# Where the Fourier branch's output weights are prepared: beside the last gates through DRAM, or at the start of attention

## The chip, the cores and the metric

The kernel runs on one core of a Trainium2 chip. The metric is the device time of one execution in microseconds. A core has TensorE (PE, matmuls), VectorE (DVE), ScalarE (ACT), GpSimd (POOL) and SyncE (SP, which here only issues transfers). Each engine works through its own list of instructions in order and waits for others on semaphores; 16 DMA engines move data between DRAM and the on-chip memory.

## The reference

One layer of a backbone block on 2048 latent tokens (a grid of 32 by 64) of 1024 channels, with 256 context tokens, in float32. Cut to what matters here:

```
fx, qx, kx, vx = split_projection(hx @ w_in)        # 4 groups of 128 channels; 8 heads of 64
y_four = fft2(fx over tokens and a group's channels, norm="ortho").real
y_attn = neighbourhood_attention(qx, kx, vx, kc, vc, rpb)   # 8 x 16 window, and all 256 context keys
g_f, g_a = split(sigmoid(hx @ w_branch_gate))
merged = g_f * (y_four @ w_fourier_out) + g_a * (y_attn @ w_attn_out)
x = x + g1 * (merged @ w_out)
x = x + g2 * (relu(hx2 @ w_mlp1) ** 2 @ w_mlp2)
```

Of the real part of a two-dimensional transform only half has to be computed: the value at (token, channel) is tied to that at the mirrored place. The kernel therefore needs w_fourier_out in two combinations, the sum and the difference of its rows with its mirrored rows. Each is split into a rounded part and the rest (H and L), so that three fast matmuls give the accuracy of a slow one.

## The kernel before

**Stages.** By the trace: the input projections, with queries, keys, values and gates (to 838 us), the Fourier transform along channels and tokens (838 to 890), attention (890 to 1214) with the Fourier branch's output product beside it, the attention branch's output product and w_out (to 1482), and the MLP (1482 to 2659).

**The gates.** `run_pair(n)` runs the projections of a pair of column blocks; the last pairs are gates. `unit_T` makes eight accumulations in PSUM (`ps_g`); ScalarE applies the sigmoid (`ot_g`, line 516, two buffers, tag "ot") and SyncE stores each result to DRAM (`gT`, line 517). Between the matmuls `turn` advances a generator, `fourier_prep`, by some steps: `pace[0]` says how many, 3 for the last pair (line 768). The generator's last part squares and sums weights (`wn`, line 883), then calls `fold(1)`.

**The Fourier stage.** `channel_dft` multiplies the channels by a folded matrix (`pc`, line 939) and splits the result (`gH`, `gL`); ScalarE's copies `gH` stand behind the last `ot_g` in its list. Matrices of the sequence transform and its input `X` are loaded by SyncE (line 814).

**Attention.** 128 blocks of 128 queries: four head pairs (hp), four row blocks (rb), four column blocks (cb), two heads (h2). Names such as `sc1_2` give the row and column block, with the head in front in the code. A block is: scores on TensorE (`sc`, lines 1303 and 1306), bias and minimum on VectorE (`s`, line 1312), the exponential on ScalarE (1316), transposes on TensorE (`tp`, 1325), two roundings (`pH` on ScalarE, 1328, `pL` on VectorE, 1333) and the product with the values (`pv`, 1339). `issue_after` fixes the order on TensorE, VectorE and ScalarE as the code is written.

**The filler.** After each block from the third on, a generator `beside_attention` is advanced one step, and a second step after every fourth block from block 16 on. It runs `merge_fourier`, then `load_wa`, and, from a fixed block on, `attn_out(0)`. `merge_fourier` first prepares the weights (`load_w`, `ws`, and the splits, lines 1183 to 1215), splits the transform's results (`ya`, `yb`), does a matmul with a single output row (`pr`), turns the row into a column (`puc`), and then does 32 accumulations of six or seven matmuls (`pmf`, line 1263), a step for every two matmuls; the results go to DRAM as `mF`, stored by GpSimd. `load_wa` loads w_attn_out in four pieces (`wao`, tag "wst" with two buffers); GpSimd scales each and splits it into `wa` (lines 1393 to 1395). `attn_out(0)` multiplies the first 256 tokens (`pua`).

**SyncE's queue.** Every load of attention goes through `fetch`, which chains it behind the one before, so that the order is that of the code:

```
    def fetch(dst, src):
        with tc.issue_after(in_order[0].ins):
            in_order[0] = sp.dma_start(dst, src)
```

`prefetch(n)` asks for the queries (`Q`, `Ql`), keys (`k`), values (`vt`) and bias tables (`bt`, issued by GpSimd, line 1091) some blocks ahead. A load that waits for its buffer holds all that stand behind it.

Of the kernel before, what the change touches and what calls it, by code (L numbers as in the profile page):

```python
# [8 lines left out]
F32 = mybir.dt.float32  # L9
# [54 lines left out]
def dit_block(ctx: ExitStack, tc: tile.TileContext, a, out, taps=None, upto=9):  # L64
# [46 lines left out]
    y64 = scratch("y64", [4, 1024])  # L111

    wfr = scratch("wfr", [4, 63, D])
    mF = scratch("mF", [8, 128, S])
    yA = scratch("yA", [4, 128, S])
    x1d = scratch("x1d", [S, D])
# [648 lines left out]
        return r  # L765

    def run_pair(n):
        pace[0] = 3 if n == len(seq) - 1 else (0, 3, 2)[min(n, 2)]
        wu, new = pair(n), [load_pair_unit(n + 1, u) for u in range(2)] if n + 1 < len(seq) else []
        js = [0, 1, "c", 2, 3] if n else [1, 2, 3]  # L770
        for j in js:
            tk = S if j == "c" else j * 512
            parts = []
            for u, (kind, _, _, i) in enumerate(seq[n]):
                if j == "c" and kind not in "kv":
                    continue
                nm = f"{kind}{i}{j}"
                if kind == "f":
                    parts.append(unit_T(wu[u], hx[j], fT, 2 * i, tk, AF.Copy, nm))
                elif kind == "g":  # L780
                    parts.append(unit_T(wu[u], hx[j], gT, 2 * i, tk, AF.Sigmoid, nm))
                elif kind in "qk":
                    parts.append(unit_qk(wu[u], hx[j], kind, 2 * i, tk, None if j == "c" else 4 * j, nm))
                else:
                    parts.append(unit_v(wu[u], hx[j], i, tk // 128, nm))
            mixed = seq[n][0][0] in "qk"
            for u, part in enumerate(parts):
                if mixed:

                    for i, _ in enumerate(part):  # L790
                        if i % 2 and len(parts) > 1:
                            next(parts[1], None)
                else:
                    for _ in part:
                        turn(0)
                if n == 0 and u == 0 and j < 3:
                    if j == 1:
                        hx[0] = first_tokens()
                    xh = [load_x(x2, ((j + 1) * 4 + i) * 128, f"{j + 1}{i}", None, i >= 2, i >= 2) for i in range(4)]
                    hx[j + 1] = build(hx_room(f"hx{j + 1}"), xh, AB, f"{j + 1}")  # L800

            for _ in range((0, 1, 2)[j] if n == 0 and j in (1, 2) else j in (0, 1, 2)):
                for o in new:
                    next(o, None)
# [61 lines left out]
    def fourier_prep():  # L866
        fold(0)
        yield
        for i in range(4):
            tH, tL = (fb.tile([128, 4, 512], F32R, tag=f"t{o}{i}", name=f"t{o}{i}") for o in "HL")  # L870
            tabs.append((tH, tL))

            tw = pa.tile([128, 4, 512], F32, tag="wst", name=f"tw{i}", bufs=2)
            sp.dma_start(tw, a["seq"][i].rearrange("(j p) m -> p j m", p=128))
            for j in range(4):
                split_on((pool, dve)[j % 2], tH[:, j], tL[:, j], tw[:, j])
                yield
            for j in (2 * i, 2 * i + 1):
                w, k = ((a["w_attn_out"][0], j), (a["w_out"][0], j - 2), (a["w_fourier_out"][0], j - 6))[(j >= 2) + (j >= 6)]
                tn = pa.tile([128, 2, D], F32, tag="wst", name=f"wn{j}", bufs=2)  # L880
                sp.dma_start(tn, w[k * 256:(k + 1) * 256, :].rearrange("(k p) n -> p k n", p=128))
                tn = tn.rearrange("p k n -> p (k n)")
                act.activation(tn, tn, AF.Square, accum_out=wn[:, j:j + 1])
                yield
        fold(1)

    for n in range(len(seq)):
        if n == 1:
# [279 lines left out]
    def merge_fourier():  # L1168
# [11 lines left out]
        ws = [pairs("wp"), pairs("wd")]  # L1180
        ys = [pairs("ya"), pairs("yb")]

        def load_w(p, fetch):
            w, wm, t = (stage(f"w{o}{p}") for o in "fms")
            for h in range(2):
                o, r0 = 64 * h, (2 * p + h) * 128
                fetch(w[o:o + 64], wf[r0:r0 + 64, :])
                pool.memset(wm[o:o + 1], 0.0)
                fetch(wm[o + 1:o + 64], wfr[2 * p + h])
            return w, wm, t  # L1190


        s64 = []
        for src in (raw(wf, 64 * D, [[128 * D, 4], [1, D]]), y64):
# [2 lines left out]
            for o in (0, 32, 64):  # L1197
                pool.dma_start(t[o:o + 4], src)
            s64.append(t)
        rows = load_w(0, fetch)  # L1200
        for p in range(2):
            for x in range(2):
                fetch(ys[x][1][:, p].bitcast(F32), yF[p][x])
        yield
        for p in range(2):
            w, wm, t = rows
            dve.tensor_tensor(out=t, in0=w, in1=wm, op=ALU.add)
            dve.tensor_tensor(out=w, in0=w, in1=wm, op=ALU.subtract)
            yield
            split_on(dve, ws[0][0][:, p], ws[0][1][:, p], t)  # L1210
            if p == 0:
                rows = load_w(1, pool.dma_start)
            yield
            split_on(dve, ws[1][0][:, p], ws[1][1][:, p], w)
            yield
            for x in range(2):
                hi, lo = (t[:, p] for t in ys[x])
                split_on(dve, hi, lo, lo.bitcast(F32))
# [645 lines left out]
```

## Time and profile before

| what | value |
|---|---|
| time, median of 3 runs | 2662.83 us (2658.7 to 2666.41) |
| the profiled execution | 2660.88 us, of it the span of the trace 2659.1 |
| mean granted TensorE clock | 0.985 |
| DMA packets, MB, mean | 345962, 517.77 MB, 195 GB/s |

The profile is of one execution. It gives the busy time of each engine, the idle time in front of an instruction with the instruction or transfer that ended it, and the windows in which the engines' busy shares can be compared. A row of the timeline reads: start in us, duration in us, engine (with a q for one that issues a transfer), line, operation, output<-input, shape, and in brackets the idle time of the engine before it and what ended it.

### The profile page before, as it was taken

The numbers are of one execution on the slowest core, as the hardware profiler recorded it, in microseconds if no ns is written. First come the engines' busy times: TensorE is split into PE (matmuls) and PEld (weight loads), VectorE is DVE, ScalarE is ACT, GpSimd is POOL, SyncE is SP. The second block draws the span as 40 slices with busy tenths as digits, with TensorE's granted clock in tenths as the row PEclk, the third lists the DMA queues.
The fourth block names the chain that finished last, engine by engine and source line by source line (L and its number), as shares of the span: only waits on it lengthen the run. The fifth ranks groups of instructions, "written<-read, shape, count | busy, mean of one in ns | idle before, by whom it ended". The sixth has DMA issues, their size and how long they took to land.

```text
span 2659.1 us, 42665 instructions
## 1 busy us (share of the span) xinstructions
PE 2538.6 (95%) x15830; PEld 1473.0 (55%) x15830; DVE 1827.3 (69%) x3672; ACT 1183.3 (44%) x2113; POOL 484.4 (18%) x715
## 2 busy tenths in 40 slices
PE   6899989898999899998999999999999999999999
PEld 5445756776656678875666444444444444444444
DVE  6756976568553678887777696978877644636367
ACT  5623225545242577874444564627351333314050
POOL 1201221012224545452000121121211100000000
PEclk9999999999999999998999999999999999999999
DMA  8577689867374744556767777787766533333334
GB/s 269 137 225 204 203 248 304 270 204 245 93 249 141 199 118 138 148 169 207 237 226 264 260 242 261 231 279 233 268 235 230 181 99 105 101 103 99 104 103 155
DMA packets 345962, 517.77 MB, mean 195 GB/s; under 512 B 48497, under 2 KB 210505, under 8 KB 341401
## 3 DMA queue, kind: packets, MB, share of 16 engines
q1 hardware_dynamic: 296425, 406.50, 48.8%
q0 software_dynamic: 29104, 75.23, 8.4%
q10 hardware_dynamic: 20224, 33.31, 3.9%
q8 instruction: 124, 2.03, 0.3%
q14 instruction: 85, 0.70, 0.1%
HBM read 370.11 MB, written 145.84 MB: 194 GB/s over the span
## 4 chain that ended last, share of the span: by engine, by line
PE 68%; DMA 11%; DVE 11%; issue 3%; ACT 3%; POOL 3%; SPq 2%; DVEq 0%; ACTq 0%; POOLq 0%
PE p L82 21%; PE pm L82 17%; PE ps_g L82 8%; PE po L82 6%; DMA w12m<-in_w_mlp 3%; PE pua L82 2%; PE ps_k L82 2%; PE tp L1325 2%; PE pmf L1263 2%; PE pv L1339 1%; SPq L188 1%; PE ps_f L82 1%; PE ps_v L82 1%; PE sc L1303 1%; DVE wo L387 1%
## 5 line engine op out<-in xcount | busy, mean ns | idle before, releaser
L82 PE MATMUL pm<-hc,wb 128*128 128x512 f16 x2688 | 582.6, 379 | 5.6 <-DVE p L1605 2.1
L82 PE MATMUL p<-wb,a 128*128 128x512 f16 x2688 | 581.9, 379 | 2.1 <-DVE X L1605 1.5
L82 PEld LDWEIGHTS <-wb 128*128 128x128 f16 x2688 | 262.9, 98 | 323.6 <-issue 7.3
L82 PEld LDWEIGHTS <-a 128*128 128x128 f16 x2688 | 263.0, 98 | 319.7 <-issue 2.9
L82 PE MATMUL ps_g<-hx,w_g 128*128 128x512 f16 x1536 | 342.5, 380 | 0.9 <-ACT ot_f L516 0.9
L1605 DVE TENSOR_TENSOR X<-X,p 128x512 f32<-128x512 f32 x280 | 184.5, 685 | 171.1 <-PE p L82 151.8
L82 PEld LDWEIGHTS <-hx 128*128 128x128 f16 x2304 | 227.4, 99 | 39.6 <-issue 7.2
L82 PEld LDWEIGHTS <-w_g 128*128 128x128 f16 x1536 | 151.0, 99 | 171.2 <-issue 3.2
L1091 POOL DMA_DIRECT2D bt<-tT x264 | 132.4, 508 | 76.3 <-DVE ri L1332 53.0
L1605 DVE TENSOR_TENSOR u<-pm,u 128x512 f32<-128x512 f32 x128 | 87.5, 690 | 84.3 <-PE pm L82 82.5
L1312 DVE CUSTOM_DVE_ANT_0 s<-sc,bt,qsc 128x736 f32<-128x736 f32 (+5 forms) x128 | 111.2, 869 | 37.1 <-PE sc L1306 33.9
L386 ACT ACTIVATE wo<-ws,msc 128x512 f16<-128x512 f32 x96 | 69.0, 718 | 152.0 <-DVE ws L430 124.0
L1609 ACT ACTIVATE p<-pm 128x512 f32<-128x512 f32 x32 | 18.9, 589 | 239.7 <-PE pm L82 239.7
L1739 POOL DMA_DIRECT2D xr<-x1d x32 | 17.3, 539 | 569.8 <-DVE X L1605 562.1
L1333 DVE SCALAR_TENSOR_TENSOR pL<-tp,pH 128x640 f16<-128x640 f32 (+1 forms) x128 | 112.3, 878 | 5.0 <-ACT pH L1328 4.5
L1316 ACT ACTIVATE s<-s,m 128x736 f32<-128x736 f32 (+5 forms) x128 | 104.6, 817 | 16.5 <-DVE m L1312 13.9
L386 ACT ACTIVATE wo<-raw,msc 128x512 f16<-128x512 f32 x128 | 87.4, 709 | 52.0 <-DVE raw L430 17.8
L82 PE MATMUL po<-wouH,mH 128*128 128x512 f16 x256 | 97.3, 384 | 9.3 <-DVE ga L1383 9.3
L1325 PE MATMUL tp<-ident,s 128*128 128x128 f32 x704 | 103.1, 281 | 0.8 <-ACT s L1316 0.7
L516 ACT ACTIVATE ot_g<-ps_g,usc_g 128x512 f32<-128x512 f32 x64 | 43.4, 681 | 130.9 <-PE ps_g L82 117.6
L82 PE MATMUL po<-wouL,mH 128*128 128x512 f16 x256 | 98.8, 386 | 2.4 <-POOL wouL L1536 2.4
L387 DVE SCALAR_TENSOR_TENSOR wo<-raw,msc,wo 128x512 f16<-128x512 f32 x128 | 94.4, 748 | 8.0 <-ACT wo L386 7.9
(535 smaller groups left out, 4645.9 us busy)
## 6 DMA issues: line engine op xcount, KB each, us to landing
wb<-w1d SPq DMA_DIRECT2D x224, 256.0 KB
wb<-w2d SPq DMA_DIRECT2D x224, 256.0 KB
w12m<-in_w_mlp SPq DMA_DIRECT2D x32, 1024.0 KB
raw<-in_w_mlp ACTq DMA_DIRECT2D x24, 1024.0 KB
w1d<-wo POOLq DMA_DIRECT2D x84, 256.0 KB, 4.0
w2d<-wo POOLq DMA_DIRECT2D x84, 256.0 KB, 4.0
gT<-ot_g SPq DMA_DIRECT2D x64, 256.0 KB
hc<-hcd SPq DMA_DIRECT2D x14, 1024.0 KB
```

What stands on the lines that cost most here:

```text
L82: last_mm[0] = pe.matmul(ps, l, r, start=(start and i == 0), stop=(stop and i == n - 1))
L188: last_load[0] = sp.dma_start(dst, src)
L386: act.activation(hi, src, AF.Copy, scale=scale)
L387: dve.scalar_tensor_tensor(out=lo, in0=src, scalar=scale, in1=hi, op0=ALU.mult, op1=ALU.subtract)
L516: act.activation(o, ps, func, scale=scale)
L1091: load_(t[i * 16:(i + 1) * 16, :, off + j0 * w:off + (j0 + 8) * w], raw(tT[ct], (2 * hp * 15 + dr) * w, [[120 * w, 16], [15 * w, 2], [1, 8 ...
L1263: pe.matmul(ps, l, r, start=(i == 0), stop=(i == len(prods) - 1))
L1312: tail["dve"] = dve.tensor_tensor_reduce(out=s[:, :n], in0=sc, in1=bias, op0=ALU.add, op1=ALU.min, scale=qsc[:, 4:5], scalar=3.0e38, accum ...
L1316: tail["act"] = act.activation(s[:, :n], s[:, :n], AF.Exp, bias=m1[:, 0:1], scale=-1.0, accum_out=m1[:, 1:2])
L1325: tail["pe"] = pe.transpose(tp[:, i * 128:(i + 1) * 128], s[:, o:o + 128], ident)
L1333: tail["dve"] = dve.scalar_tensor_tensor(out=pL[:, :c], in0=tp[:, :c], scalar=PTOP, in1=pH[:, :c], op0=ALU.mult, op1=ALU.subtract)
L1605: last["dve"] = dve.tensor_tensor(out=o, in0=x, in1=y, op=op)
```

## The change

The preparation of the weights moves out of `merge_fourier` into `fourier_prep`, behind `fold(1)`: for each p (two of the four groups) the loads of `w_fourier_out` and of its mirrored rows (`wfr`, `wm`), the memset of the row that has no mirror, sum and difference, and the two splits. The results go to a new DRAM tensor `wfD`, eight stores of 0.5 MB. In attention four loads of 1 MB bring them back, in the place of the loads of `wf` and `wm`. `pace[0]` of the last pair is 4 instead of 3, and the filler has six steps fewer. The numerical work is the same.

```diff
--- before.py
+++ after.py
@@ -111,6 +111,8 @@
     y64 = scratch("y64", [4, 1024])
 
     wfr = scratch("wfr", [4, 63, D])
+
+    wfD = scratch("wfD", [2, 2, 2, 128, D])
     mF = scratch("mF", [8, 128, S])
     yA = scratch("yA", [4, 128, S])
     x1d = scratch("x1d", [S, D])
@@ -765,7 +767,7 @@
         return r
 
     def run_pair(n):
-        pace[0] = 3 if n == len(seq) - 1 else (0, 3, 2)[min(n, 2)]
+        pace[0] = 4 if n == len(seq) - 1 else (0, 3, 2)[min(n, 2)]
         wu, new = pair(n), [load_pair_unit(n + 1, u) for u in range(2)] if n + 1 < len(seq) else []
         js = [0, 1, "c", 2, 3] if n else [1, 2, 3]
         for j in js:
@@ -883,6 +885,26 @@
                 act.activation(tn, tn, AF.Square, accum_out=wn[:, j:j + 1])
                 yield
         fold(1)
+        yield
+
+        for p in range(2):
+            w, wm = (pa.tile([128, KT, 256], F32, tag="wst", name=f"w{o}{p}", bufs=2).rearrange("p k n -> p (k n)") for o in "fm")
+            t, w = w[:, D:], w[:, :D]
+            for h in range(2):
+                o, r0 = 64 * h, (2 * p + h) * 128
+                sp.dma_start(w[o:o + 64], a["w_fourier_out"][0][r0:r0 + 64, :])
+                pool.memset(wm[o:o + 1, :D], 0.0)
+                sp.dma_start(wm[o + 1:o + 64, :D], wfr[2 * p + h])
+            dve.tensor_tensor(out=t, in0=w, in1=wm[:, :D], op=ALU.add)
+            dve.tensor_tensor(out=w, in0=w, in1=wm[:, :D], op=ALU.subtract)
+            yield
+            for x, src in enumerate((t, w)):
+                o = pa.tile([128, 2, KT, 256], F16, tag="w", name=f"wfo{p}{x}", bufs=4).bitcast(F32R)
+                o = o.rearrange("p o k n -> p (o k n)").rearrange("p (o n) -> p o n", o=2)
+                split_on(dve, o[:, 0], o[:, 1], src)
+                for i in range(2):
+                    sp.dma_start(wfD[x, i, p], o[:, i].bitcast(F32))
+                yield
 
     for n in range(len(seq)):
         if n == 1:
@@ -1180,15 +1202,6 @@
         ws = [pairs("wp"), pairs("wd")]
         ys = [pairs("ya"), pairs("yb")]
 
-        def load_w(p, fetch):
-            w, wm, t = (stage(f"w{o}{p}") for o in "fms")
-            for h in range(2):
-                o, r0 = 64 * h, (2 * p + h) * 128
-                fetch(w[o:o + 64], wf[r0:r0 + 64, :])
-                pool.memset(wm[o:o + 1], 0.0)
-                fetch(wm[o + 1:o + 64], wfr[2 * p + h])
-            return w, wm, t
-
 
         s64 = []
         for src in (raw(wf, 64 * D, [[128 * D, 4], [1, D]]), y64):
@@ -1197,22 +1210,14 @@
             for o in (0, 32, 64):
                 pool.dma_start(t[o:o + 4], src)
             s64.append(t)
-        rows = load_w(0, fetch)
         for p in range(2):
             for x in range(2):
                 fetch(ys[x][1][:, p].bitcast(F32), yF[p][x])
+        for x in range(2):
+            for i in range(2):
+                fetch(ws[x][i].bitcast(F32), wfD[x, i].rearrange("a p n -> p a n"))
         yield
         for p in range(2):
-            w, wm, t = rows
-            dve.tensor_tensor(out=t, in0=w, in1=wm, op=ALU.add)
-            dve.tensor_tensor(out=w, in0=w, in1=wm, op=ALU.subtract)
-            yield
-            split_on(dve, ws[0][0][:, p], ws[0][1][:, p], t)
-            if p == 0:
-                rows = load_w(1, pool.dma_start)
-            yield
-            split_on(dve, ws[1][0][:, p], ws[1][1][:, p], w)
-            yield
             for x in range(2):
                 hi, lo = (t[:, p] for t in ys[x])
                 split_on(dve, hi, lo, lo.bitcast(F32))
```

The last gates, on SyncE, in the changed kernel. `wm` is a load of mirrored rows for p=1, `gT` a store of a gate result, `wfD` a store of finished weights; before, the last loads of `wn` were followed by nothing but the gate stores.

```order
L519 DMA gT<-ot_g_0_8725 128x512
L906 DMA wfD<-wfo_8888 128x1024 x2
L897 DMA wm_8894<-wfr 63x1024 x2
L519 DMA gT<-ot_g_1_8757 128x512
L519 DMA gT<-ot_g_0_8790 128x512
L906 DMA wfD<-wfo_8931 128x1024
L906 DMA wfD<-wfo_8936 128x1024
L906 DMA wfD<-wfo_8931 128x1024
L906 DMA wfD<-wfo_8936 128x1024
L519 DMA gT<-ot_g_1_8842 128x512
L519 DMA gT<-ot_g_0_8885 128x512
L519 DMA gT<-ot_g_1_8928 128x512
```

The four stores of p=1 stand between the gate stores, ahead of the last three. On ScalarE the copies of p=0 and p=1 (`wfo`) stand between the gate results, in the changed kernel:

```order
L518 ACTIVATE ot_g_1_8688<-ps_g_1_8663,usc_g_7661 128x512
L87 ACTIVATE wfo_8855<-wf_8845 128x1024
L87 ACTIVATE wfo_8888<-wf_8845 128x1024
L518 ACTIVATE ot_g_0_8725<-ps_g_0_8700,usc_g_7665 128x512
L518 ACTIVATE ot_g_1_8757<-ps_g_1_8732,usc_g_7665 128x512
L518 ACTIVATE ot_g_0_8790<-ps_g_0_8765,usc_g_7661 128x512
L87 ACTIVATE wfo_8931<-wf_8893 128x1024
L87 ACTIVATE wfo_8936<-wf_8893 128x1024
L518 ACTIVATE ot_g_1_8842<-ps_g_1_8817,usc_g_7661 128x512
L518 ACTIVATE ot_g_0_8885<-ps_g_0_8860,usc_g_7665 128x512
L518 ACTIVATE ot_g_1_8928<-ps_g_1_8903,usc_g_7665 128x512
L87 ACTIVATE gH_0_8961<-pc_0_8969 128x4x64
```

Before, the eight gate results stood together, with nothing but the squares of `wn` between the first of them.

The start of attention, on VectorE, before: `s` and `m` are a block's bias and minimum, `pL` its second rounding, the two digits the row and column block.

```order
L1333 SCALAR_TENSOR_TENSOR pL_0_1_9582<-tp_0_1_9575,pH_0_1_9581 128x640
L1207 TENSOR_TENSOR ws_9456<-wf_9454,wm_9455 128x1024
L1029 TENSOR_SCALAR g1r<-g1r,mgs 128x1024
L1312 ISA s_9429,m_0_2_9628<-sc_0_2_9623,bt_9319,qsc 128x608
L1312 ISA m_0_2_9628 128x1
L1332 RECIPROCAL ri_0_1_9630<-m_0_1_9543 128x1
L1333 SCALAR_TENSOR_TENSOR pL_0_1_9621<-tp_0_1_9614,pH_0_1_9620 128x640
L1208 TENSOR_TENSOR wf_9454<-wf_9454,wm_9455 128x1024
L90 TENSOR_TENSOR wpL<-ws_9456,wpH 128x1024
L1312 ISA s_9430,m_0_3_9685<-sc_0_3_9680,bt_9319,qsc 128x520
L1312 ISA m_0_3_9685 128x1
L1332 RECIPROCAL ri_0_2_9687<-m_0_2_9589 128x1
```

And in the changed kernel, from the same block on:

```order
L1338 SCALAR_TENSOR_TENSOR pL_0_1_9618<-tp_0_1_9611,pH_0_1_9617 128x640
L1051 TENSOR_SCALAR g1r<-g1r,mgs 128x1024
L1317 ISA s_9470,m_0_2_9664<-sc_0_2_9659,bt_9360,qsc 128x608
L1317 ISA m_0_2_9664 128x1
L1337 RECIPROCAL ri_0_1_9666<-m_0_1_9579 128x1
L90 TENSOR_TENSOR yaL<-yaL,yaH 128x1024
L1338 SCALAR_TENSOR_TENSOR pL_0_1_9657<-tp_0_1_9650,pH_0_1_9656 128x640
L1317 ISA s_9471,m_0_3_9712<-sc_0_3_9707,bt_9360,qsc 128x520
L1317 ISA m_0_3_9712 128x1
L1337 RECIPROCAL ri_0_2_9714<-m_0_2_9625 128x1
L90 TENSOR_TENSOR ybL<-ybL,ybH 128x1024
L1338 SCALAR_TENSOR_TENSOR pL_0_2_9705<-tp_0_2_9698,pH_0_2_9704 128x640
```

The sum, the difference and the splits `wpL` and `wdL` are gone from here, and the splits of `ya` and `yb` have moved up to their place.

The last head pair, on SyncE, before (`Q_1_0` is row block 1, head 0):

```order
L1051 DMA Q_1_0_14190<-qH 64x512 x2
L1051 DMA Ql_1_0_14193<-qL 64x512 x2
L1051 DMA Q_1_1_14196<-qH 64x512 x2
L1051 DMA Ql_1_1_14199<-qL 64x512 x2
L1051 DMA vt_3_14208<-v_63 24x2048 x4
L1051 DMA wao_14398<-in_w_attn_out 128x1024
L1051 DMA wao_14403<-in_w_attn_out 128x1024
L1051 DMA wao_14408<-in_w_attn_out 128x1024
L1051 DMA wao_14413<-in_w_attn_out 128x1024
L1051 DMA Q_2_0_14577<-qH 64x512 x2
L1051 DMA Ql_2_0_14580<-qL 64x512 x2
```

And in the changed kernel:

```order
L1073 DMA vt_1_14043<-v_63 32x2048 x4
L1073 DMA vt_2_14134<-v_63 32x2048 x4
L1073 DMA wao_14189<-in_w_attn_out 128x1024
L1073 DMA wao_14194<-in_w_attn_out 128x1024
L1073 DMA wao_14199<-in_w_attn_out 128x1024
L1073 DMA wao_14204<-in_w_attn_out 128x1024
L1073 DMA Q_1_0_14246<-qH 64x512 x2
L1073 DMA Ql_1_0_14249<-qL 64x512 x2
L1073 DMA Q_1_1_14252<-qH 64x512 x2
L1073 DMA Ql_1_1_14255<-qL 64x512 x2
L1073 DMA vt_3_14264<-v_63 24x2048 x4
L1073 DMA Q_2_0_14592<-qH 64x512 x2
```

The four loads of w_attn_out now stand ahead of the queries of row block 1 and of `vt_3`, not behind them. On GpSimd fifteen bias loads stand between the last `mF` store and the first operation on `wao`, where five stood before.

## The prediction

> **What bounds the kernel now.** I read the page first: the share of the engines, and the chain that ended last.
>
> ```profile
> PE 2538.6 (95%) x15830; PEld 1473.0 (55%) x15830; DVE 1827.3 (69%) x3672; ACT 1183.3 (44%) x2113; POOL 484.4 (18%) x715
> PE 68%; DMA 11%; DVE 11%; issue 3%; ACT 3%; POOL 3%; SPq 2%; DVEq 0%; ACTq 0%; POOLq 0%
> ```
>
> TensorE is busy for 95% of the span, so only stretches in which it idles can give anything, and every new wait of TensorE is paid in full. To find these stretches I asked for busy time by window around the three places that the change touches.
>
> ```profile
> 760.00:800.00 40.00, 40.00 (x188) 18.30 (x187) 21.78 (x35) 17.18 (x26) 14.12 (x10) 1.00 0.94 322
> 820.00:840.00 20.00, 20.00 (x108) 10.78 (x106) 0.00 (x0) 3.69 (x7) 2.77 (x2) 1.00 0.14 53
> 900.00:920.00 20.00, 14.20 (x183) 11.31 (x182) 19.92 (x44) 16.98 (x35) 12.13 (x22) 1.00 0.92 234
> 920.00:940.00 20.00, 12.22 (x169) 9.73 (x168) 19.70 (x33) 16.60 (x35) 6.01 (x12) 0.97 0.38 94
> 940.00:945.00 5.00, 5.00 (x33) 3.17 (x32) 2.83 (x8) 3.35 (x7) 2.75 (x6) 0.50 0.09 17
> 960.00:1140.00 180.00, 179.08 (x2215) 147.34 (x2214) 150.66 (x335) 143.52 (x329) 94.72 (x193) 1.00 0.54 152
> ```
>
> The columns after the window and its length are the busy time of TensorE, its weight loads, VectorE, ScalarE and GpSimd, then granted clock, DMA share and GB/s. At the last gates (820 to 840) VectorE does nothing and the DMA engines are at 0.14. At the start of attention (900 to 940) VectorE is busy for 39.6 of 40 us and TensorE for 26.4. From 960 to 1140 TensorE is full again. So the change takes work from a place where VectorE is the bound to one where it is free. That is a true gain; the question is what its transfers meet.
>
> **The change part by part. (a) The start of attention.** Eight VectorE operations go. These are the second and third of them, and what TensorE did meanwhile (sc opens a block's scores; pr is the first matmul of the filler):
>
> ```profile
> 906.31 1.22 DVE L1208 TENSOR_TENSOR wf<-wf,wm 128x1024 f32<-128x1024 f32 x1
> 907.44 1.22 DVE L90 TENSOR_TENSOR wpL<-ws,wpH 128x1024 fp32r<-128x1024 f32 x1
> 919.29 0.36 PE L1303 MATMUL sc<-k,Q 128*128 128x480 f16 x1
> 921.26 0.36 PE L1303 MATMUL sc<-k,Q 128*128 128x480 f16 x1
> 934.27 0.31 PE L1303 MATMUL sc<-k,Q 128*128 128x360 f16 x1 [0.86 <-DVE m L1312]
> 937.52 0.40 PE L82 MATMUL pr<-wpH,cH 128*1 128x512 f32 x1
> 937.76 0.39 PE L82 MATMUL pr<-wpL,cH 128*1 128x512 f32 x1
> 945.27 0.46 PE L1303 MATMUL sc<-k,Q 128*128 128x480 f16 x1
> ```
>
> Two of them that follow one another start 1.13 us apart (906.31, 907.44), so eight are 9 us of VectorE. Block 16 opens at 934.27, block 18 at 945.27: 11 us for two blocks that cost TensorE at most 1.97 us each (919.29 to 921.26), at half clock for part of it (0.50 in 940 to 945). The filler has seven row matmuls in them, at 0.24 us each (937.52 to 937.76) some 1.6 us; that leaves 5.7 lost. In the order of the changed kernel the row matmuls stand already behind blocks 11 and 12, so by block 16 TensorE has fourteen of them, eight small transposes and some six matmuls of the merge behind it, 5.3 us at the same 0.24, and block 16 comes at about 933, limited by TensorE rather than VectorE. Together: 1.2 earlier, 5.3 of work already done, 5.7 not lost, 12 us.
>
> Against it stands SyncE's queue, which issues in order:
>
> ```profile
> 889.81 0.50 SPq L1051 DMA_DIRECT2D wf<-in_w_fourier_out  x1
> 891.96 0.34 SPq L1051 DMA_DIRECT2D yaL<-yF  x1
> 895.02 1.10 SPq L1051 DMA_DIRECT2D Q<-qH  x2
> 904.58 2.92 SPq L1051 DMA_DIRECT2D Ql<-qL  x2
> 900.00:903.00 3.00, 3.00 (x38) 2.37 (x37) 3.00 (x14) 2.93 (x8) 1.98 (x4) 1.00 1.08 340
> 909.40 0.27 PE L1303 MATMUL sc<-k,Q 128*128 128x264 f16 x1 [1.69 <-DVE m L1312]
> ```
>
> Before the first Q load stood 1 MB of wf and wm and 2.1 MB of y; now 2.1 MB of y and 4.2 MB of finished weights. At the 340 GB/s of 900 to 903 the 6.3 MB take 18.5 us from about 890, so Q for block 8 lands near 911 to 912, and the second half some 3 us later. The block is due near 909.7 (before it was block 7 that opened at 909.40; the queue of VectorE is now shorter). I take 3 us of stall; its ends are 0 (if block 8 is itself late by as much) and 8 (at the 234 GB/s of the window 900 to 920). **Gain 9 us, 4 to 13.**
>
> One rule speaks against the change here. The Trainium skill, "DMA: Bandwidth & Descriptors", section "Issuing engines are not separate DMA queues", says that transfers of SyncE, ScalarE and GpSimd end on the same 16 engines and interleave; by it the bias loads that GpSimd issues are delayed by the 4.2 MB too. The share of 1.08 at 900 to 903 agrees with that. It is the third rival below.
>
> **(b) The end of the gates.** What stands there now, ScalarE, SyncE and VectorE:
>
> ```profile
> 811.82 1.91 ACT L883 ACTIVATE wn<-wn 128x2048 f32<-128x2048 f32 x1 [2.77 <-DMA wn<-in_w_fourier_out]
> 816.95 0.69 ACT L516 ACTIVATE ot_g<-ps_g,usc_g 128x512 f32<-128x512 f32 x1 [1.97 <-DMA gT<-ot_g]
> 837.25 0.69 ACT L516 ACTIVATE ot_g<-ps_g,usc_g 128x512 f32<-128x512 f32 x1 [4.49 <-PE ps_g L82]
> 838.04 0.38 ACT L87 ACTIVATE gH<-pc 128x256 fp32r<-128x256 f32 x1
> 809.07 29.21 SPq L517 DMA_DIRECT2D gT<-ot_g  x8
> 840.22 0.16 DVE L949 COPY col<-pss 128x2 f32<-128x2 f32 x1 [33.59 <-PE pss L948]
> ```
>
> VectorE idles for 33.59 us before 840.22, so the eight operations themselves are hidden, and so are four ScalarE copies. What is not hidden is the order. In the changed kernel the two ScalarE copies of p=1 stand ahead of the last three gate outputs (ot_g), and four wfD stores of 0.5 MB ahead of the last three gate stores on SyncE. The ot buffers are two, so the last gate output waits until the third last store has landed; a wait of this kind is already there (816.95, 1.97 us on a gT store). Step by step, with 1.13 us for an operation and 322 GB/s (760 to 800) for a stream: wf and wm of p=0 are issued around 809 and 814 and landed by 818.5; add, subtract and two splits end at 823.3; only then are their two buffers free for p=1, and wm of p=1 goes out at 826.4 behind stores of 1.5 MB, landing near 834.5; its four operations end at 840; the last wfD store goes out at 840.5, the gate store behind it at 841, and with 2.3 MB ahead since 838 it lands near 846.5. The last gate output follows, and the first gH copy of the Fourier stage, 838.04 before, comes at about 847. TensorE has four banks for gates and is not held, but its next matmuls need gH. **Cost 9 us, 3 to 11**: 3 is what such a wait costs already (1.97) and one output more (0.69); 11 comes out at the 234 GB/s of 900 to 920 for the 2.3 MB ahead of wm.
>
> **(c) The last head pair.** The merge has six filler steps fewer, so its last matmul (pmf) stands in block 96 and not in block 100, and w_attn_out's loads (wao) come earlier in SyncE's queue: ahead of Q for row block 1 and vt_3, not behind them. What they cost there now:
>
> ```profile
> 1143.08 17.69 SPq L1051 DMA_DIRECT2D wao<-in_w_attn_out  x4
> 1145.97 2.55 POOL L1091 DMA_DIRECT2D bt<-tT  x5
> 1148.55 5.69 POOL L1393 TENSOR_SCALAR wao<-wao,mgs 128x1024 f32<-128x1024 f32 x2
> 1154.18 2.02 POOL L1394 CAST waH<-wao 128x1024 f16<-128x1024 f32 x2
> 1156.17 4.24 POOL L1395 TENSOR_TENSOR waL<-wao,waH 128x1024 f16<-128x1024 f32 x2
> 1160.87 1.09 SPq L1051 DMA_DIRECT2D Q<-qH  x2
> 1163.32 1.19 SPq L1051 DMA_DIRECT2D Q<-qH  x2
> 1165.60 0.31 PE L1303 MATMUL sc<-k,Q 128*128 128x360 f16 x1 [1.89 <-DMA Q<-qH]
> 1148.73 0.32 PE L1303 MATMUL sc<-k,Q 128*128 128x360 f16 x1
> 1150.37 0.31 PE L1303 MATMUL sc<-k,Q 128*128 128x360 f16 x1
> 1183.59 0.27 PE L82 MATMUL pua<-yaL,waH 128*128 128x256 f16 x1 [1.93 <-POOL yaL L1366]
> ```
>
> SyncE stands for 17.69 us at the four loads, because the third and fourth wait for buffers that GpSimd frees after 12 us of work (1148.55 to 1160.4). The Q behind them is 1.89 us late even so. Count from the end of the last pmf, t. Before, GpSimd began at t+5.4 (1148.55), behind five bias loads; now fifteen stand there, ten more at 0.51 us, so t+10.5. The fourth wao load leaves at t+22.7, the first Q behind it, and its block opens 4.7 us after that Q's issue (1160.87, 1165.60): t+27.5. Blocks without filler are 1.64 us apart (1148.73, 1150.37), so block 104 is due after seven of them at t+11.5. That is a stall of 16 us. vt_3 goes out behind eight Q loads of about 1.2 us and lands near t+33, and the products of block 102 need it: some 4 us more; and TensorE is at half clock after so long a gap (as 940 to 945), 1 us. Of these 21 the present kernel pays about 6 (1.89, the 2.7 before the output products, 1183.59 among them, and the slow clock after): **cost 15, 4 to 20.** The low end stands for a GpSimd whose bias loads are out before t. The Trainium skill, "TensorE: Matmul & The Clock Gate", section "Part 1: The HAM clock gate", says that the clock halves after an idle window of about 3.4 us and needs as long of work to come back; by its figures an estimate of the last item would be 1.7 us. The granted 0.50 of 940 to 945 agrees.
>
> **(d) Smaller parts.** The output products (pua) begin in block 112 and not 119, so loads for the next tile are asked for sooner; behind attention VectorE waits 1.42 us for such a load:
>
> ```profile
> 1215.85 0.69 DVE L1376 TENSOR_TENSOR ft<-ft,gf 128x512 f32<-128x512 f32 x1 [1.42 <-DMA ft<-mF]
> ```
>
> I take 1.4 us of gain, 0 to 4. The MLP is untouched: nothing. The faster pace of the generator beside the last gates moves VectorE and ScalarE work under full TensorE: nothing, and at most the 3.69 us that ScalarE does at 820 to 840 if that cover were gone.
>
> **Sum.** The profiled execution took 2660.9 us (span 2659.1). 2660.9 + 9 - 9 + 15 - 1.4 = 2674.5. The three timed runs have a median 2 us above it, so **2676 us** beside a median of 2662.83.
>
> **The rivals.** *First, faster:* the last stores do not hold the gates and the queue at the last head pair is not late, so only the gain is left. The mechanism is GpSimd's: if it has finished the first two wao tiles before t+6.5, which is 16 us sooner than worked out, SyncE is free when Q is due, and the stall of (c) goes, the 1.89 of now with it. Then 2660.9 + 3 - 9 - 3 = 2652, 2654 by the median. For it: the bias loads could be out before the last pmf. Against it: the last mF store, which stands ahead of them on GpSimd, needs that pmf. It decides from a stall of about 3 us in (c) downward. Chance 0.12.
>
> *Second, no change:* each cost at its low end, 2660.9 + 3 - 9 + 4 = 2659, 2661 by the median. For it: TensorE has other work in the filler, and VectorE's and ScalarE's backlog could be what block 104 waits for. Against: 1.89 us are late already with Q in a better place. Chance 0.18.
>
> *Third, crowded transfers:* by the rule of shared engines the start of attention gains 4 and not 9, and the gate stores come later too: 2660.9 + 11 - 4 + 20 = 2688, 2690 by the median. For it: the share of 0.92 over 900 to 920. Against: the rates of 340 GB/s in between. Chance 0.2.
>
> *Fourth,* that the weights are not made beside the gates at all is excluded by the order, where they stand there.
>
> **How the numbers follow.** The forecast has 0.5. The range goes from 2656, between the first two rivals, to 2690, the third. A difference of 0.3%, 8 us, is what can be told from no change. Slower by more (over 2671): forecast and third rival, 0.7. Faster by more (under 2655): the first, 0.12. Between: 0.18.
>
> **What would show it.** Right: gH of the first Fourier group about 9 us later than the end of the last gate matmul, with a gT store named as ot_g's releaser; pr near block 11 and VectorE no longer full from 920 to 940; four wao loads on SyncE ahead of Q, over 20 us long, and a gap of TensorE of over 10 us in front of a score matmul, released by Q. Wrong: gH as soon as before, or no gap at row block 1 of the last head pair; then the time is near the first or second rival.

## The result, and the profile after

The changed kernel took 2686.46 us (median of three runs, 2686.04 to 2686.97) beside 2662.83 us before: a ratio of 1.0088, 95% interval 1.0067 to 1.0110. It is slower by 23.6 us. Taken once more, with five runs, it had a median of 2678.45 us beside 2663.01, a ratio of 1.0055 (1.0041 to 1.0069): slower by 15.4 us. 35 runs of the kernel before lay between 2647.8 and 2669.9 us, so single executions of one kernel differ by some 20 us; below, times are compared as medians or ratios over several runs, and single traces cut by cut.

First the busy time by window of the changed kernel, with the columns as before:

```profile
820.00:840.00 20.00, 20.00 (x95) 9.04 (x94) 4.80 (x4) 6.06 (x8) 3.91 (x6) 1.00 0.68 229
840.00:860.00 20.00, 12.97 (x75) 10.99 (x74) 10.45 (x23) 6.40 (x14) 16.12 (x20) 0.73 0.50 179
900.00:920.00 20.00, 14.91 (x131) 9.98 (x130) 14.79 (x49) 11.85 (x24) 10.69 (x19) 0.91 0.86 308
920.00:940.00 20.00, 14.85 (x170) 11.47 (x171) 16.70 (x33) 16.04 (x35) 8.56 (x17) 0.91 0.76 203
960.00:1140.00 180.00, 179.21 (x2211) 147.78 (x2209) 150.41 (x333) 144.98 (x330) 91.93 (x187) 1.00 0.53 150
1140.00:1160.00 20.00, 13.53 (x198) 11.74 (x196) 13.91 (x34) 13.93 (x36) 15.82 (x23) 0.91 0.47 145
1160.00:1180.00 20.00, 8.71 (x88) 7.01 (x89) 5.23 (x13) 4.79 (x11) 17.78 (x10) 0.58 0.43 125
```

VectorE is no longer full from 900 to 940 (31.5 of 40 us, not 39.6), as was meant. The price is in two other windows: TensorE idles for 7 us in 840 to 860, and for 18 us in 1140 to 1180, where the granted clock falls to 0.58 as well.

The first of them, by ScalarE, SyncE, VectorE and TensorE in the timeline:

```profile
841.92 1.23 DVE L898 TENSOR_TENSOR wf<-wf,wm 128x1024 f32<-128x1024 f32 x1 [10.57 <-DMA gT<-ot_g]
843.18 1.06 ACT L87 ACTIVATE wfo<-wf 128x1024 fp32r<-128x1024 f32 x1 [5.60 <-DVE wf L898]
845.40 1.25 ACT L518 ACTIVATE ot_g<-ps_g,usc_g 128x512 f32<-128x512 f32 x2
851.96 0.69 ACT L518 ACTIVATE ot_g<-ps_g,usc_g 128x512 f32<-128x512 f32 x1 [5.31 <-DMA gT<-ot_g]
852.55 0.92 ACT L87 ACTIVATE gH<-pc 128x256 fp32r<-128x256 f32 x3
844.27 2.92 SPq L906 DMA_DIRECT2D wfD<-wfo  x4
847.28 5.71 SPq L519 DMA_DIRECT2D gT<-ot_g  x3
853.86 7.06 PE L961 MATMUL pc<-chan,fold 128*128 128x64 f32 x32 [7.03 <-DVE gL L90]
```

ScalarE waits 5.60 us for the sum of p=1, puts out two gate results late, and then waits 5.31 us for a gate store that stands behind the four wfD stores on SyncE (844.27, then 847.28). gH follows at 852.55; the last gate matmul had ended at 843.8. These 8.7 us were 0.9 before.

The second, on SyncE, GpSimd and TensorE:

```profile
1140.39 25.89 SPq L1073 DMA_DIRECT2D wao<-in_w_attn_out  x4
1166.33 1.09 SPq L1073 DMA_DIRECT2D Q<-qH  x2
1150.11 3.97 POOL L1113 DMA_DIRECT2D bt<-tT  x8 [2.17 <-DMA mF<-mo]
1154.12 5.67 POOL L1398 TENSOR_SCALAR wao<-wao,mgs 128x1024 f32<-128x1024 f32 x2
1171.29 0.46 PE L1308 MATMUL sc<-k,Q 128*128 128x360 f16 x1 [17.46 <-DMA Q<-qH]
```

SyncE stands for 25.89 us at the four loads, and block 104 waits 17.46 us for the Q behind them. In the row of 960 to 1140 TensorE is busy as long as before, to 0.1 us: nothing is lost between.

**Where the 25 us between the two traces lie.** The traces are cut at the same instructions: the end of the last gate matmul, the first gH copy, and the first score matmul of blocks 0, 103, 111 and 127. The table has the difference from the trace before, in us.

| kernel | to the last gate matmul | to gH | to block 0 | to block 103 | to block 111 | to block 127 | to the end | sum |
|---|---|---|---|---|---|---|---|---|
| after | +6.6 | +7.9 | -1.1 | -8.5 | +20.2 | +3.3 | -3.3 | +25.2 |
| after, again | +4.2 | +8.5 | +1.0 | -9.2 | +19.1 | +2.6 | -3.4 | +22.8 |

The first column is not the change's. The lists of all engines are the same in both kernels up to 806 us, TensorE's up to block 7 of attention, and the two differences stand already at the first matmul of the last pair of gates (760.3 and 757.9 us, 753.7 before), ahead of all that moved. The 33rd of the 64 gate results came anywhere between 566.6 and 576.1 us in fourteen traces of kernels with and without the change. The other columns add up to +18.5 and +18.6. The trace before is one execution too: in runs seven and eleven below, where an edit of the kernel before lies behind these stretches, the one to block 0 came out 0.1 and 3.3 us shorter and the one to block 103 1.5 and 1.8 us shorter. So a column is good to some 2 or 3 us.

### The profile page after: what moved, and what is told of

It is laid out like the page before. It is cut to its first block, busy times and chain, and to the rows that moved or that the text cites. A ratio compares the mean times of both kernels' runs of the same rounds, so it can differ in the third digit from the quotient of the medians.

```text
span 2684.3 us, 42694 instructions
## 1 busy us (share of the span) xinstructions
PE 2544.6 (95%) x15830; PEld 1479.6 (55%) x15830; DVE 1826.4 (68%) x3672; ACT 1182.5 (44%) x2113; POOL 481.8 (18%) x711
## 4 chain that ended last, share of the span: by engine, by line
PE 68%; DVE 11%; DMA 11%; ACT 3%; issue 2%; SPq 2%; POOL 2%; DVEq 0%; ACTq 0%; POOLq 0%
PE p L82 20%; PE pm L82 18%; PE ps_g L82 8%; PE po L82 6%; DMA w12m<-in_w_mlp 4%; PE pua L82 2%; PE tp L1330 2%; PE ps_k L82 2%; PE pmf L1268 2%; PE pv L1344 2%; SPq L190 1%; PE sc L1308 1%; DVE wo L389 1%; PE ps_f L82 1%; DMA Ql<-qL 1%
## 5 line engine op out<-in xcount | busy, mean ns | idle before, releaser
L82 PEld LDWEIGHTS <-hx 128*128 128x128 f16 x2304 | 228.4, 100 | 40.2 <-issue 7.5
L388 ACT ACTIVATE wo<-raw,msc 128x512 f16<-128x512 f32 x128 | 87.4, 710 | 51.6 <-issue 18.5
L82 PE MATMUL po<-wouH,mL 128*128 128x512 f16 x256 | 98.6, 385 | 0.0
```

Source lines behind the costliest of these rows:

```text
L82: last_mm[0] = pe.matmul(ps, l, r, start=(start and i == 0), stop=(stop and i == n - 1))
L388: act.activation(hi, src, AF.Copy, scale=scale)
```

## The experiments

**One: the loads of w_attn_out behind Q again.**

```diff
         yield from merge_fourier()
+        for _ in range(6):
+            yield
```

> The changed kernel, with six empty filler steps put between the merge and the loads of w_attn_out, so that these stand behind Q of row block 1 and vt_3 on SyncE again. Theory (the place in SyncE's queue makes the stall of the last head pair): the gap of 17.46 us in front of block 104 goes, a late Q of about 2 us comes back at row block 2, and the time falls by 15 to 19 us, to about 2669. Rival (the stall comes from GpSimd's later bias loads or from transfers, wherever wao stands in the queue): a gap of over 10 us stays and the time stays above 2680.

Measured: 2664.33 us, 1.0007 of the kernel before (0.9991 to 1.0022), some 5 us below the time expected. The gap in front of block 104 is gone, the one at row block 2 is longer than it was:

```profile
1171.19 0.46 PE L1308 MATMUL sc<-k,Q 128*128 128x360 f16 x1 [5.53 <-DMA Q<-qH]
```

It is 5.53 us and not 1.89; fifteen bias loads still stand ahead of GpSimd's work, where five stood before. Between blocks 103 and 111 the difference is 0.0 where it was 20.2. The place in the queue makes the large stall; with the place as before and GpSimd later, 3.6 us more than before are left here (1.6 in run twelve, which has the same order).

**Two: the same order in the kernel before.**

```diff
-            step(block(hp, rb, cb, h2, yp), (n >= 2) + (n >= 8 and (2 * n + h2) % 4 == 0))
+            step(block(hp, rb, cb, h2, yp), (n >= 2) + (n >= 8 and (2 * n + h2) % 4 == 0) + (40 <= 2 * n + h2 < 46))
```

> The kernel before, with six filler steps more in blocks 40 to 45, where TensorE is full: the merge ends four blocks earlier and the loads of w_attn_out come ahead of Q of row block 1, and nothing of the weights' preparation is touched. Theory: the stall of the last head pair appears in this kernel too, over 10 us in front of block 104 and released by Q, and the time rises by 15 to 19 us, to about 2680. Rival (the stall needs the later start of attention or the extra transfers): within 4 us of 2663.

Measured: 2674.49 us, 1.0051 (1.0031 to 1.0071). The stall is there, without any of the change:

```profile
1166.60 0.46 PE L1303 MATMUL sc<-k,Q 128*128 128x360 f16 x1 [15.00 <-DMA Q<-qH]
```

+17.0 us between blocks 103 and 111, and -1.2 from there to the end. The theory expected 15 to 19 in all; the trace has 15.8 behind block 103, the times 12. What the change did here was to take six steps out of the filler, nothing else.

**Three and four: what holds the gates.** Three moves the stores to GpSimd. Four moves the loads there too, and the rounded halves to VectorE:

```diff
-                sp.dma_start(w[o:o + 64], a["w_fourier_out"][0][r0:r0 + 64, :])
+                pool.dma_start(w[o:o + 64], a["w_fourier_out"][0][r0:r0 + 64, :])
...
-                sp.dma_start(wm[o + 1:o + 64, :D], wfr[2 * p + h])
+                pool.dma_start(wm[o + 1:o + 64, :D], wfr[2 * p + h])
...
-                split_on(dve, o[:, 0], o[:, 1], src)
+                split_on(dve, o[:, 0], o[:, 1], src, dve)
                 for i in range(2):
-                    sp.dma_start(wfD[x, i, p], o[:, i].bitcast(F32))
+                    pool.dma_start(wfD[x, i, p], o[:, i].bitcast(F32))
```

> The changed kernel with the eight stores of finished weights issued by GpSimd and not by SyncE; loads, copies and all else as they were. Theory (the stores ahead of the gate stores on SyncE are half of the delay, the rest is the loads of p=1 and the ScalarE copies ahead of the gate results): the first gH copy comes 5 to 7 us sooner than at 852.55 and the time falls by as much, to about 2680. Rival (only loads and copies hold the gates): gH at most 2 us sooner, time above 2684.

> The changed kernel with loads and stores of the weights beside the gates all issued by GpSimd, and the rounded halves made by VectorE instead of ScalarE, so that neither SyncE's nor ScalarE's list holds anything of them between the gate results. Theory (the delay of the Fourier stage is one of order on these two engines, not of the work or the transfers): gH comes at 838 to 841 as before the change and the time falls by 11 to 14 us, to about 2673. Rival (the 4 MB of stores and 2 MB of loads slow the gate stores by themselves): gH after 846 and a time above 2680.

Measured: 2678.22 us (1.0068, 1.0043 to 1.0094) and 2677.53 us (1.0068, 1.0043 to 1.0093). ScalarE in run three, then in run four:

```profile
843.64 0.69 ACT L518 ACTIVATE ot_g<-ps_g,usc_g 128x512 f32<-128x512 f32 x1 [1.27 <-DMA gT<-ot_g]
844.23 0.92 ACT L87 ACTIVATE gH<-pc 128x256 fp32r<-128x256 f32 x3
```

```profile
841.83 0.69 ACT L518 ACTIVATE ot_g<-ps_g,usc_g 128x512 f32<-128x512 f32 x1 [4.49 <-PE ps_g L82]
842.62 0.39 ACT L87 ACTIVATE gH<-pc 128x256 fp32r<-128x256 f32 x1
```

By absolute time gH in run three comes 8.3 us sooner than in the changed kernel, but its last gate matmul also ended 6.3 us sooner; counted from that matmul, gH is at 6.8 and not 8.7. So the stores alone are worth 2 us (2.6 beside the second trace of the changed kernel), less than expected (5 to 7): the loads of p=1 and the copies ahead of the gate results hold most of it; the two were not tried apart. In run four the last gate result is released by the matmul, as before the change, and gH follows 0.9 us after that matmul (at 842.62, not by 841, since the matmul itself ended 4.6 us later than before): the loss is one of order on SyncE and ScalarE, whole. The 4 MB of stores and 2 MB of loads cost nothing there. (From block 0 to block 103 run four gains 6.9 us and not 8.5; whether GpSimd's later start on its bias tables is the cause was not tried.)

The traces of three and four differ as they should (the stage from the gates to gH is 5.9 us shorter in four), but run four's time is not the 2673 expected, and the medians of four and five runs do not show the difference; at spreads of 7 and 11 us they can't. Run three's 2678 us is near the 2680 expected, but so is the changed kernel's second median. The medians of ten to twelve runs do show run four's edit: it takes 5.5 us from run nine (run ten) and 4.1 from run one (run twelve), less than the stage's 8.

**Five to seven: the loads of w_attn_out from GpSimd.** Five is run four with this edit; six puts the two loads of wdH and wdL behind the filler's first step as well; seven is the kernel before with the edit alone.

```diff
-            fetch(wt, a["w_attn_out"][0, k * 128:(k + 1) * 128, :])
+            pool.dma_start(wt, a["w_attn_out"][0, k * 128:(k + 1) * 128, :])
```

> The changed kernel with the weights beside the gates off SyncE's and ScalarE's lists (as in the run before) and the four loads of w_attn_out issued by GpSimd, which also uses them, so that SyncE never stands at them. Theory (the change gains 8 to 9 us at the start of attention, and both losses are waits in SyncE's order): the gap in front of block 104 is under 2 us, gH follows the last gate matmul within 1 us, and the time is 6 to 12 us below the kernel before. Rival (GpSimd's 24 us of work on w_attn_out, now begun later, makes the output products wait instead): the time is no better than that of the kernel before, with a gap of over 8 us in front of the first pua.

> The run before this one, with the two loads of the difference's weights (wdH, wdL, 2 MB) put behind the Q loads of row block 1, so that 2 MB less stand ahead of them at the start of attention. Theory (the late Q at block 8 costs some 3 us of the gain): the wait for Q in front of block 8, 2.43 us in the changed kernel, goes, and the time falls by another 2 to 4 us. Rival (VectorE's work and the shared DMA engines set the pace there, and the Q is late beside other waits): within 1 us of the run before it.

> The kernel before with only the four loads of w_attn_out issued by GpSimd: what that edit is worth without the change. Theory: the late Q of row block 2 (1.89 us) goes and the time falls by 1 to 4 us. Rival (GpSimd ends later by the landing of its loads, some 4 us, and the output products wait for it): no change, or up to 4 us slower.

Measured: five 2660.17 us, 0.9987 (0.9978 to 0.9996); six 2663.2 us, 1.0000 (0.9988 to 1.0011); seven 2668.39 us, 1.0019 (1.0010 to 1.0028). The gap at block 104 is gone in five, but the output products now wait. Below is their first matmul in the kernel before, in five and in seven:

```profile
1181.39 0.27 PE L82 MATMUL pua<-yaH,waH 128*128 128x256 f16 x1 [0.80 <-ACT yaH L1365]
```

```profile
1180.82 0.37 PE L82 MATMUL pua<-yaH,waH 128*128 128x256 f16 x1 [6.05 <-ACT yaH L1370]
```

```profile
1189.97 0.37 PE L82 MATMUL pua<-yaH,waH 128*128 128x256 f16 x1 [7.81 <-ACT yaH L1365]
```

The load that GpSimd issues it then waits for itself, which delays its own 24 us of work: counted from the last pmf, that work ends at 46.1 us in five and at 38.9 in four, at 40.2 in seven and at 30.9 before; and yat shares the buffers that it frees. So the rival holds in seven, which came out 5 us slower, a little more than the 4 it allowed. In five it holds in part: between blocks 111 and 127 five loses 4.1 us and seven 7.7 (2.4 in run four, without this edit), and five is 3 us below the kernel before, not 6 to 12. Run six was expected 2 to 4 us below five and came out 3 above. It shows that the late Q at block 8 is no term of its own: its wait is gone from the trace (3.25 us in five), and the stretch from block 0 to block 103 is the same, -7.1 us in both.

**Eight: the changed kernel again.**

> The changed kernel itself once more. Of the 25 us between the two traces 6.6 stand ahead of anything that the change touches (the last gate matmul ends at 843.8 and not at 837.2). If these are scatter between executions, the last gate matmul ends at 837 to 840 here, and the median is 16 to 20 us above the kernel before; if they belong to the change, it ends after 842 again and the difference stays at 23 to 26 us.

The last gate matmul ended at 841.4, between the two expected cases, and the last pair of gates began already 4.2 us later than in the trace before; the median is 15.4 us above the kernel before, just under the lower case. By the table the terms of the change repeat to about 2 us; the first column, which is no term of it, went from 6.6 to 4.2.

**Nine to eleven: four buffers under the tag of w_attn_out's loads,** in the changed kernel, in run four, and in the kernel before.

```diff
-            wt = pm.tile([128, D], F32, tag="wst", name=f"wao{k}", bufs=2)
+            wt = pm.tile([128, D], F32, tag="wst", name=f"wao{k}", bufs=4)
...
-        yt = pm.tile([128, D], F32, tag="wst", name=f"yat{t}", bufs=2).rearrange("p (k t) -> p k t", k=4)
+        yt = pm.tile([128, D], F32, tag="wst", name=f"yat{t}", bufs=4).rearrange("p (k t) -> p k t", k=4)
...
-        t = p_.tile([128, D], F32, tag=tag, name=f"wou{k}", bufs=2)
+        t = p_.tile([128, D], F32, tag=tag, name=f"wou{k}", bufs=2 + 2 * (k % 2 == 0))
```

> The changed kernel with four buffers instead of two under the tag of w_attn_out's loads (which the loads of yat and wou share), and nothing else: the loads stand ahead of Q as in the changed kernel, but none has to wait for GpSimd. Theory (SyncE stands there because the third and fourth load wait for a buffer): the four loads take under 4 us on SyncE, the gap in front of block 104 is under 2 us, and the time falls by 17 to 22 us from the changed kernel's, to within 6 us of the kernel before. Rival (the 2 MB of the loads, or GpSimd's later bias loads, make the Q late): a gap of over 8 us stays.

> Four buffers, and the weights beside the gates off SyncE's and ScalarE's lists: both losses gone by the two single edits, only the gain left. Theory (the terms add up: gain of 9 us, losses of 8 and 18): 8 us below the run with four buffers alone, and 7 to 14 us below the kernel before. Rival (what is no longer waited for in one place is waited for in the next, as with GpSimd's loads): at most 3 us below the kernel before.

> The kernel before with the four buffers alone: what they are worth without the change. Theory: the late Q of row block 2 (1.89 us) and part of the 2.7 us in front of the first output products go, and w_out's loads come sooner behind attention: 2 to 8 us faster. Rival: within 1 us of the kernel before, since the first wait is for GpSimd's work and not for a buffer.

Measured: 2668.61 us (1.0026, 1.0014 to 1.0038), 2663.16 us (1.0009, 0.9995 to 1.0022) and 2659.26 us (0.9988, 0.9978 to 0.9999). In run nine, SyncE, TensorE, and from the view of waits SyncE's longest:

```profile
1137.59 1.78 SPq L1073 DMA_DIRECT2D wao<-in_w_attn_out  x4
1140.56 11.67 SPq L1073 DMA_DIRECT2D Ql<-qL  x2
1154.38 0.46 PE L1308 MATMUL sc<-k,Ql 128*128 128x360 f16 x1 [3.20 <-DMA Ql<-qL]
```

```profile
SPq L1073 <- DMA yA<-yo: 10.6, 1, 10.6
```

The four loads take 1.78 us, so the wait at them was the buffers. But SyncE then stands 10.6 us in front of the second half of Ql until a store of ScalarE (yA) has landed, and 6.0 us of the 20 between blocks 103 and 111 stay (8.5 in run ten). Nine's theory is right on the four loads and on the gap in front of block 104; a late Q stays all the same, as the rival had it, though the wait is 3.20 us and not over 8.

The store was issued after that wait had begun:

```profile
1144.48 0.33 ACTq L1358 DMA_DIRECT2D yA<-yo  x1
```

The semaphore records of the trace show what ties the two. The transfers of SyncE and ScalarE report their landing on the same eight semaphores in turn, and by these records a transfer waits until the earlier one on its semaphore has landed. The second half of Ql got the semaphore that yA had been given, whose turn came just ahead of the four loads. SyncE began to wait at 1141.2; ScalarE came to the store only 3.3 us later, and its landing took 7.3 us. The same wait, on a yA store, is there in run ten (9.9 us) and in run eleven (10.4, of them 8.0 until the issue and 2.4 for the landing).

Ten's theory fails: it is 5.5 us below nine, not 8, and not below the kernel before, as its rival said. Eleven's theory holds at its low end, 3 us: in its trace no block of row block 2 waits for Q.

**Twelve: run four with the six empty steps.**

> The two fixes that need no memory: the weights beside the gates off SyncE's and ScalarE's lists, and six empty filler steps ahead of w_attn_out's loads. By the run with the six steps alone (1.0007 of the kernel before) less the 8 us between the last gate matmul and gH, the time is 5 to 9 us below the kernel before. Rival (the Fourier stage's 8 us are given back at the start of attention, where the Q loads would then be later against their blocks): within 3 us of it.

Measured: 2660.23 us, 0.9995 (0.9984 to 1.0007). By the cuts nothing is lost any more at the gates (0.0) or between blocks 103 and 111 (0.0), and 8.8 us are gained from block 0 to block 103; the wait for Q at row block 2 is 3.46 us, the stretch from gH to block 0 was 2.4 us longer, and the part ahead of the last gate matmul 4.3. Without that last part its trace is 6.7 us below that of the kernel before. The times show 2, with an interval that reaches zero: as little as the rival said, though not by its path, since the gain at the start of attention is there. A gain from the change with its losses undone is thus likely by the trace and not shown by the times. Only runs five and eleven are below the kernel before with an interval that ends below 1, both by 0.1%, and eleven has nothing of the change: four buffers alone gave as much.

## Why the prediction was right, and which term was off

The forecast was slower, 2676 us in a range of 2656 to 2690. The measured 2686.46 us lies inside, 10 us above the forecast; the second measurement, 2678.45, is 2 us above it. In the trace 6.6 of these 10 us lie ahead of the last pair of gates, where the change does nothing; that the first time is so far up is no part of the mechanism. Of the terms, without that part:

- *Start of attention, 9 us of gain (4 to 13).* The cuts from block 0 to 103 show 8.5 and 9.2. pr stood in blocks 11 and 12, where the order had it, and VectorE was no longer full. Blocks 16 and 17 took 5.0 us and not 11.0, and by block 18 the gain was 4.1 us; the rest came behind it, where the filler's work was already done. (By its own rows the 5.7 us lost in those two blocks are 5.4.) The stall for Q at block 8 was 2.43 us, 3 were taken; that it costs these 3 us by itself is not so, by run six.
- *End of the gates, 9 us of loss (3 to 11).* Measured 7.9 and 8.5. gH came at 852.55 and not 847 because the whole stage ended 6.6 us later in that execution. The mechanism, a gate store behind wfD stores and ScalarE's copies ahead of the gate results, is in the rows above, and run four takes it away whole. The weights of its parts were not as thought: the stores are 2 of the 8.
- *The last head pair, 15 us of loss, with 1.4 of gain behind it.* The gross stall was foreseen at 21: 16 in front of block 104, 4 for vt_3, 1 for the clock. Measured: 17.46, and 20.2 and 19.1 up to block 111. No wait for vt_3 shows in the changed kernel's rows. The slow clock took its place: blocks 104 and 105 took 3.0 us each and not 1.64, 2.7 us in all (below: the score matmuls of blocks 105 and 106, behind 104 at 1171.29, and the granted clock, third number from the right). That the gross sum came out within 2 us is partly luck: 4 us for vt_3 were not paid, and the gap and the clock took 1.5 and 1.7 more than was put down for them. The Trainium skill, "TensorE: Matmul & The Clock Gate", section "Part 1: The HAM clock gate", puts the return to full speed after at least one busy window of some 3.4 us. In this trace the clock came back 5.5 us after block 104 had opened, between 1176 and 1177, so the 1 us of the sum was too little.

```profile
1174.29 0.51 PE L1308 MATMUL sc<-k,Q 128*128 128x360 f16 x1
1177.28 0.37 PE L1308 MATMUL sc<-k,Q 128*128 128x480 f16 x1
1171.00:1176.00 5.00, 4.71 (x38) 3.50 (x38) 1.88 (x5) 1.80 (x4) 5.00 (x4) 0.50 0.53 148
1176.00:1177.00 1.00, 1.00 (x15) 1.00 (x13) 1.00 (x4) 0.40 (x2) 1.00 (x1) 0.58 0.29 93
1177.00:1178.00 1.00, 1.00 (x13) 0.76 (x11) 0.45 (x1) 1.00 (x3) 1.00 (x2) 1.00 0.40 118
```

**The step that failed** is the credit in (c): "Of these 21 the present kernel pays about 6", and with it the 1.4 us of (d). These 6 us did not come back. From block 111 to the end the two columns are +3.3 and -3.3. Between blocks 111 and 127, first before, then after, TensorE idles as long:

```profile
1161.76:1206.74 44.98, 39.68 (x520) 34.22 (x518) 37.40 (x83) 33.23 (x75) 19.34 (x11) 0.96 0.49 154
1186.86:1235.18 48.32, 42.66 (x538) 36.81 (x536) 42.51 (x94) 34.59 (x78) 7.26 (x5) 0.96 0.51 163
```

That is 5.3 us of idle time before and 5.7 after, at a granted clock of 0.96 in both. The late Q of row block 2 and the wait for the output products are gone, and in their place TensorE waits for VectorE, which is busy for 42.5 of 48.3 us and not 37.4 of 45.0. The products of the first tile now stand between blocks 112 and 122 and no longer between 119 and 127. Run two, where the filler alone moved, has the same waits for VectorE there; why VectorE is late at just these blocks was not tried. The rows in the changed kernel:

```profile
1202.87 0.36 PE L1308 MATMUL sc<-k,Q 128*128 128x480 f16 x1 [1.65 <-DVE m L1317]
1224.02 0.66 PE L1355 MATMUL ty<-ident,yp 128*128 128x128 f32 x4 [0.82 <-DVE ga L1388]
1231.22 0.26 PE L1344 MATMUL pv<-vt,pL 128*128 128x64 f16 x3 [1.86 <-DVE pL L1338]
```

With 20 in place of 13.6 the sum is 2660.9 + 9 - 9 + 20 = 2681, beside 2679.4 from the cuts without their first column (2660.9 + 18.5).

The rivals: that GpSimd might be ready before block 104 was due did not happen. It began its work at 1154.12, 13.5 us after the last pmf (1140.6) where 10.5 were worked out; among the bias loads it waited 2.17 us for the landing of mF, which the sum had left out. The Q left at t+25.7 for 22.7, and block 104 was due at t+13.2 (1171.29 less 17.46) for 11.5: later by 3.0 and 1.7 us, so that most of the two errors cancelled and the stall came out near the forecast, which is luck too. The second rival had each cost at its low end; the last head pair was at its high end. The third rival did not happen either, though the first measured time lies near its 2690: the start of attention gained 8.5 and 9.2 us, not 4, and in run four the stores and loads beside the gates cost nothing. Transfers that delay one another show in a place where it was not looked for, in run nine. The Trainium skill, "DMA: Bandwidth & Descriptors", section "Issuing engines are not separate DMA queues", has transfers of all issuers interleave on the same engines. Run nine agrees: from 1140 to 1149, with 2 MB of w_attn_out and 1 MB of mF under way, the DMA share was 1.00, and the yA store that SyncE waited for, among them, took 7.3 us to land; in run eleven, where the share had fallen to 0.33 when the store was issued, it took 2.4.

## What to carry to other kernels

An edit that takes steps out of a filler moves everything that comes behind it in the filler; here that cost 17 us in the trace without any other part of the change (run two), twice what the edit gained at the start of attention. So look where a program's other loads land in an in-order queue, and whether one of them waits there for a buffer that a slow engine frees. Work put beside an idle engine was not free here as long as its copies, loads and stores stood ahead of the results of the stage it was put beside; with loads and stores on GpSimd and the copies on VectorE, which both had little else to do there, the wait was gone (run four). And a wait that goes is worth only what the next wait leaves of it: two wao buffers gave way to a store's landing, a late Q to VectorE.

## What the runs showed of the hardware that was not expected

With four buffers SyncE stood 10.6 us in front of a Q load until a store issued by ScalarE had landed, though that load does not read what the store writes. The two share one of eight landing semaphores, so that a load of SyncE can wait for a store which ScalarE has not even issued: 3.3 us of the wait in run nine, 8.0 in run eleven. And the part of the program ahead of the last gates takes up to 9.5 us more or less from one execution to the next (33rd gate result at 566.6 to 576.1 us), which is as much as the terms that were to be measured; the cuts at equal instructions show a term to some 2 or 3 us where the times of five runs do not.
